# A hybrid decoder step on one core: the tanh-GELU of its state-space branch with the cubic constant inside ScalarE's square, and one VectorE instruction where two instructions stood

## The chip, the core and the metric

The program runs on one core of a Trainium2 chip: TensorE (PE in the profile; its weight loads are PEld), VectorE (DVE), ScalarE (ACT), GpSimd (POOL), and SyncE (SP), which issues most of the transfers. The metric is the device time of one execution in microseconds, lower is better. A difference of 0.2%, about 6 us, is what a measurement of this kernel can just tell from no change.

## The reference, cut to what matters

The reference is one layer of a decoder over a prompt of 2048 tokens and 32 sample tokens (8 sequences of 4). A combined projection feeds two branches, a diagonal state-space branch (S5) and a retention branch. Both feed an output projection; a memory cross-attention and a squared-ReLU MLP follow. The change concerns the activation of the state-space branch, the tanh form of GELU:

```python
y = y.reshape(bsz, L, SSM_WIDTH) + d_skip.astype(F32) * uf
z = jax.nn.gelu(y)
out = z * jax.nn.sigmoid(z @ w_glu.astype(F32))
```

With x the branch's output, GELU is 0.5 x (1 + tanh(0.798 (x + 0.044715 x³))). The kernel holds x/4 in the tile `yS`, so the inner term is built as y · (1 + 0.044715 (4y)²) and scaled by 4 · 0.798 in the tanh.

## The kernel before

The prompt is cut into four blocks of 512 tokens; the sample tokens ride along in the second block, whose tiles are 544 columns wide. The program first runs a **mixer phase** over the four blocks (block 0 to block 3 in what follows), then the attention and MLP phase over the same blocks. Every large matrix product is made of three fp32r products with the operands split into a high and a low part. Weights come in as `raw`, ScalarE copies out the high part and VectorE or GpSimd computes the low part (both go into the tile `whl`), and the product lands in a PSUM tile `dn`.

In the mixer phase each block has four groups of channels in its S5 branch, called batches here, so 16 in all. A batch (`s5_batch`) transposes its input to `u4`, multiplies by the matrices `q4` (PSUM tiles `vr`, `vi`), rotates the products on VectorE and GpSimd (tiles `t0`, `t1`, `gl`, which the profile shows as `t` and `gl`), runs two scans (`Yr`, `Yi`), rotates back, and multiplies by `pm4` into the PSUM tile `py`. ScalarE evicts `py`, TensorE transposes it (`pf`), ScalarE writes `yS`, and `s5_gelu` is started. Its tile `gl = mb(..., "yT")` is called `yT` in the profile. Its last two steps split the result into the tile `z`.

Beside the S5 batches run the four retention heads of the block: projections evicted as `qr`, `kr`, `gate` on VectorE and GpSimd, a transpose `pkd`, scores `psc`, the state product `pkv`, the output `po`, normalised in `scs`, and a transpose `pt`. The retention of the sample tokens, one head after the other, uses the small tiles `rsc`, `px`, `po2`, `pn` (the products `pn` update the sample state; `rsc` is their masked operand, built on GpSimd). Each engine runs its instructions in the order written.

That order is not written out by hand: the program carries a small planner (`Model`, `Order`). It keeps a clock per engine, adds for each instruction a start cost and a cost per column, and lets side jobs (`s5_chain`, `s5_gelu`, `retention`, `ret_sample`) go on when its clock says that they are due; `yield "sg1"` and the like give the offset in ns by which a job waits after its own last instruction. With the key set to 2, `E("x_g1")` gives the instruction to whichever of VectorE and GpSimd the planner thinks is free first. So an instruction less in a side job moves that job's due time, and with it the place of other jobs' instructions on all engines.

Of the kernel before, what the change touches and what calls it, by code (L numbers as in the profile page):

```python
# [13 lines left out]
AF = mybir.ActivationFunctionType  # L14
ALU = mybir.AluOpType
# [313 lines left out]
def tile_decoder_step(ctx: ExitStack, tc: tile.TileContext, ins: dict, outs: dict):  # L329
    nc = tc.nc  # L330
    model = Model()
    V, A, G, SY = (Engine(model, e, k) for e, k in ((nc.vector, "V"), (nc.scalar, "A"), (nc.gpsimd, "G"), (nc.sync, "SP")))
    T = nc.tensor

    def E(key):
        return Either(model, (V, G), key)
# [73 lines left out]
    def zact():  # L410
        return com.tile([P, 2, TM_], F32R, tag="z", name="z", bufs=4)
# [51 lines left out]
    def split(dst, src, scale=None):  # L463

        split_first(dst, src, scale)
        split_rest(dst, src, scale)
# [564 lines left out]
    def mb(shape, tag, bufs=1, dt=F32):  # L1031
        return pt("mixb", shape, tag, bufs, dt)
# [271 lines left out]
    def s5_batch(B, be, mats, nxt):  # L1304
# [82 lines left out]
        if sample:  # L1387
# [12 lines left out]
            for tt_ in range(4):  # L1400
                tr(pfs[:, tt_ * NB:(tt_ + 1) * NB], yTs[:, tt_].rearrange("p a b -> p (a b)"), ident[:NB, :NB])
            A.activation(yS[:, :, P:], pfs[:, :4 * NB].rearrange("p (a b) -> p a b", a=4), AF.Copy)
        M["gelu"] = od.spawn(s5_gelu(B, yS), yS)

    def s5_gelu(B, yS):
        t = B["t"]
        y = yS[:, :, :t // 4]
        gl = mb((P, 4, TM_ // 4), "yT")[:, :, :t // 4]
        A.activation(gl, y, AF.Square, scale=4.0)
        E("x_g1").tensor_scalar(gl, gl, 0.044715, 1.0, op0=ALU.mult, op1=ALU.add)  # L1410
        E("x_g2").tensor_tensor(out=gl, in0=gl, in1=y, op=ALU.mult)
        yield "sg1"
        A.activation(gl, gl, AF.Tanh, scale=4.0 * 0.7978845608028654)
        yield "sg2"
        V.scalar_tensor_tensor(out=gl, in0=gl, scalar=1.0, in1=y, op0=ALU.add, op1=ALU.mult)
        while B["b"] and "glu" not in blk[B["b"] - 1]:
            yield 300
        z = zact()
        split(z[:, :, :t].rearrange("p s (a b) -> p s a b", a=4), gl)
        B["z"].append(z)  # L1420
# [954 lines left out]
```

## Time and profile before

| | |
|---|---|
| device time, median of 3 runs | 3053.83 us (3050.05 to 3056.23) |
| the profiled execution: its time, and its span from first to last instruction | 3057.99 us, 3055.8 us |
| PE busy | 2944.5 us, 96% of the span |
| DVE, POOL, ACT busy | 1767.3 us, 1314.5 us, 1007.1 us |
| TensorE's granted clock over the span | 0.988 |

Busy shares are averages over phases with different limits: TensorE is the bound of the whole, and what the other engines do matters where TensorE waits for them. The mixer phase, in which all 16 GELUs lie, ends at about 960 us.

### The profile page before, as it was taken

What the parts mean: (1) busy time and instruction counts of PE and PEld (TensorE: products, weight loads), DVE (VectorE), ACT (ScalarE), POOL (GpSimd) and SP (SyncE); (2) the same over time, 40 slices, a digit from 0 to 9 for tenths busy, and PEclk for the clock granted to TensorE, in tenths of its full rate; (3) what the DMA queues carried; (4) which work ended last, traced back from release to release, by engine and by line L of the source; (5) the groups of instructions that cost most, each with busy time, mean ns of one, the idle gap of its engine ahead of it and who ended that gap; (6) DMA issues with size and microseconds to landing.
All of it is one profiled execution on the core that took longest, in us unless ns stands there. A gap on an engine that the chain in (4) does not pass through costs nothing.

```text
span 3055.8 us, 43238 instructions
## 1 busy us (share of the span) xinstructions
PE 2944.5 (96%) x16676; PEld 2561.3 (84%) x16676; DVE 1767.3 (58%) x3088; ACT 1007.1 (33%) x1440; POOL 1314.5 (43%) x1463
## 2 busy tenths in 40 slices
PE   8898899998989999999999999999999999999998
PEld 6688788877987978888987888788999998978887
DVE  8968858779675654334465555556533444553334
ACT  4442232322454332223333333433322223432222
POOL 5534434344565153334534344462433326153334
PEclk9999999999999999999999999999999999999999
DMA  5453253342685222234324444542222233232222
GB/s 151 137 171 111 83 154 119 115 156 75 230 269 168 90 93 95 96 97 141 114 88 145 145 149 148 198 134 83 91 84 90 90 132 122 81 99 94 96 90 76
DMA packets 138957, 374.37 MB, mean 123 GB/s; under 512 B 18656, under 2 KB 39808, under 8 KB 138752
## 3 DMA queue, kind: packets, MB, share of 16 engines
q1 hardware_dynamic: 138176, 371.10, 37.3%
q8 instruction: 131, 2.15, 0.3%
q14 instruction: 74, 0.61, 0.1%
q10 hardware_dynamic: 576, 0.52, 0.1%
HBM read 334.17 MB, written 37.40 MB: 122 GB/s over the span
## 4 chain that ended last, share of the span: by engine, by line
PE 65%; DVE 1%; issue 0%; DMA 0%; ACT 0%; POOL 0%; POOLq 0%; SPq 0%; ACTq 0%; DVEq 0%
PE dn L447 57%; PE sc L447 6%; PE zps L447 1%; DVE rst L197 1%; PE ptp L451 0%; PE st L447 0%; DVE rsy L197 0%; DMA raw<-in_w_down 0%; DVE act L197 0%; PE sp L447 0%; POOL x L197 0%; DVE mx L197 0%; ACT x L197 0%; DVE stage L197 0%; DVE ms L197 0%
## 5 line engine op out<-in xcount | busy, mean ns | idle before, releaser
L447 PE MATMUL dn<-actl,whl 128*128 128x512 f32 (+2 forms) x4656 | 916.3, 356 | 2.2 <-DVE x L197 2.2
L447 PE MATMUL dn<-act,whl 128*128 128x512 f32 (+2 forms) x4704 | 913.3, 348 | 2.1 <-POOL whl L197 1.6
L197 POOL TENSOR_TENSOR whl<-raw,whl 128x256 fp32r<-128x256 f32 x896 | 692.7, 805 | 510.8 <-ACT whl L197 494.3
L447 PEld LDWEIGHTS dn<-actl,whl 128*128 128x128 f32 x4656 | 767.7, 188 | 130.5 <-ACT whl L197 1.9
L447 PEld LDWEIGHTS dn<-act,whl 128*128 128x128 f32 x4704 | 752.7, 189 | 110.8 <-issue 3.0
L197 ACT ACTIVATE whl<-raw 128x1024 fp32r<-128x1024 f32 (+1 forms) x505 | 523.2, 1046 | 650.7 <-PE dn L447 460.5
L197 DVE TENSOR_TENSOR x<-dn,x 128x512 f32<-128x512 f32 (+2 forms) x496 | 291.4, 606 | 430.7 <-PE dn L447 430.2
L197 DVE TENSOR_TENSOR whl<-raw,whl 128x1024 fp32r<-128x1024 f32 (+1 forms) x281 | 400.0, 1429 | 174.3 <-ACT whl L197 164.2
L447 PE MATMUL dn<-z,whl 128*128 128x512 f32 (+1 forms) x2160 | 435.1, 352 | 0.0
L447 PEld LDWEIGHTS dn<-z,whl 128*128 128x128 f32 x2160 | 353.4, 188 | 56.5 <-issue 1.1
L197 POOL TENSOR_TENSOR actl<-sq,actl 128x512 fp32r<-128x512 f32 (+1 forms) x128 | 171.2, 1338 | 455.0 <-DVE sq L197 445.4
L197 DVE SCALAR_TENSOR_TENSOR relu<-dn,rb 128x512 f32<-128x512 f32 (+1 forms) x160 | 91.6, 589 | 323.4 <-PE dn L447 316.0
L197 ACT ACTIVATE actl<-relu 128x512 fp32r<-128x512 f32 (+1 forms) x128 | 82.2, 642 | 512.5 <-DVE relu L197 512.5
L447 PE MATMUL dn<-whl,act 128*128 128x512 f32 x768 | 203.0, 413 | 11.6 <-ACT whl L197 6.3
L197 POOL TENSOR_TENSOR acc<-acc,relu 128x512 f32<-128x512 f32 (+2 forms) x77 | 107.4, 1394 | 237.1 <-ACT relu L197 235.0
L447 PEld LDWEIGHTS dn<-whl,act 128*128 128x128 f32 x768 | 168.0, 255 | 35.9 <-ACT whl L197 7.0
L197 DVE TENSOR_TENSOR sq<-relu 128x512 f32<-128x512 f32 (+1 forms) x128 | 91.6, 715 | 14.8 <-POOL actl L197 2.3
L447 PE MATMUL sc<-whl,act 128*128 128x256 f32 x576 | 80.3, 291 | 14.2 <-ACT p L197 9.4
L447 PEld LDWEIGHTS sc<-whl,act 128*128 128x128 f32 x576 | 75.1, 197 | 15.6 <-ACT p L197 10.0
L447 PE MATMUL sc<-whl,z 128*128 128x256 f32 x576 | 80.8, 291 | 0.0
L197 DVE SCALAR_TENSOR_TENSOR act<-x,small,act 128x512 fp32r<-128x512 f32 (+2 forms) x76 | 64.4, 854 | 28.2 <-ACT act L197 28.2
L197 ACT ACTIVATE act<-x,small 128x512 fp32r<-128x512 f32 (+2 forms) x76 | 53.0, 701 | 72.8 <-DVE x L197 52.9
(318 smaller groups left out, 2671.8 us busy)
## 6 DMA issues: line engine op xcount, KB each, us to landing
raw<-in_w_up SPq DMA_DIRECT2D x128, 512.0 KB, 3.5
raw<-in_w_down SPq DMA_DIRECT2D x128, 512.0 KB, 3.5
raw<-in_w_out SPq DMA_DIRECT2D x32, 512.0 KB, 3.5
raw<-wq_d SPq DMA_DIRECT2D x32, 512.0 KB, 3.5
raw<-wo_d SPq DMA_DIRECT2D x32, 512.0 KB, 3.5
x<-in_xT SPq DMA_DIRECT2D x48, 256.0 KB, 4.3
pm<-pm_d SPq DMA_DIRECT2D x16, 768.0 KB, 5.3
tab<-tab_d SPq DMA_DIRECT2D x16, 516.0 KB, 4.4
```

The lines of the kernel that those rows point to most:

```text
L197: return f(*args, **kw)
L447: T.matmul(out, lhsT, rhs, start=start, stop=stop)
```

## The change

ScalarE's square takes the scale 4·√0.044715 in place of 4, so that it gives 0.044715 (4y)². The multiply-add by a tensor-scalar instruction and the multiplication by y, two instructions that the planner gives to VectorE or GpSimd, become one VectorE instruction, (square + 1) · y.

```diff
@@ s5_gelu
         gl = mb((P, 4, TM_ // 4), "yT")[:, :, :t // 4]
-        A.activation(gl, y, AF.Square, scale=4.0)
-        E("x_g1").tensor_scalar(gl, gl, 0.044715, 1.0, op0=ALU.mult, op1=ALU.add)
-        E("x_g2").tensor_tensor(out=gl, in0=gl, in1=y, op=ALU.mult)
+        A.activation(gl, y, AF.Square, scale=4.0 * 0.044715 ** 0.5)
+        V.scalar_tensor_tensor(out=gl, in0=gl, scalar=1.0, in1=y, op0=ALU.add, op1=ALU.mult)
         yield "sg1"
         A.activation(gl, gl, AF.Tanh, scale=4.0 * 0.7978845608028654)
```

By the change 16 instructions go, 13 of them on VectorE and 3 on GpSimd. In the planner's new order the engines' programs are the same up to about 217 us and from about 960 us on; between them the order differs in places. Three of those follow.

The first place is VectorE and TensorE in the first S5 batch of block 1. The rows of VectorE before, from the rotation of `vr` to the scans (the second `SCALAR_TENSOR_TENSOR yT` is (tanh + 1)·y):

```order
L197 TENSOR_TENSOR gl<-vr,tab 128x4x128
L197 TENSOR_SCALAR yT<-yT 128x544
L197 TENSOR_TENSOR yT<-yT,yS 128x544
L197 TENSOR_TENSOR t_4392<-vi,tab 128x4x128
L197 COPY Yr<-carr 128x4
L197 COPY Yi<-cari 128x4
L197 TENSOR_TENSOR kr<-dn,cosr 128x512
L197 TENSOR_TENSOR tmp<-dn,sinr 64x512 x2
L197 SCALAR_TENSOR_TENSOR yT<-yT,yS 128x544
L197 TENSOR_TENSOR z<-yT,z 128x544
L197 SCALAR_TENSOR_TENSOR Yr<-rho_86,carr,t_4391 128x128 x4
```

VectorE now:

```order
L197 TENSOR_TENSOR gl<-vr,tab 128x4x128
L197 SCALAR_TENSOR_TENSOR yT<-yT,yS 128x544
L197 TENSOR_TENSOR t_4388<-vi,tab 128x4x128
L197 COPY Yr<-carr 128x4
L197 COPY Yi<-cari 128x4
L197 SCALAR_TENSOR_TENSOR yT<-yT,yS 128x544
L197 TENSOR_TENSOR z<-yT,z 128x544
L197 TENSOR_TENSOR kr<-dn,cosr 128x512
L197 TENSOR_TENSOR tmp<-dn,sinr 64x512 x2
L197 SCALAR_TENSOR_TENSOR Yr<-rho_86,carr,t_4387 128x128 x4
```

The end of the GELU has moved ahead of the eviction of `kr`. On TensorE the same stretch, one piece of the difference:

```order
-L447 MATMUL dn<-act,whl 128x512 x36
-L451 MATMUL pkd<-ident,kr 128x128 x4
-L447 MATMUL psc<-qr,kr 128x128 x4
-L447 MATMUL dn<-act,whl 128x512 x6
+L447 MATMUL dn<-act,whl 128x512 x39
+L451 MATMUL pkd<-ident,kr 128x128 x4
+L447 MATMUL psc<-qr,kr 128x128 x4
+L451 MATMUL pu<-ident,tm_3965 128x128 x4
+L447 MATMUL dn<-act,whl 128x512 x6
```

Three more of the projection's matmuls stand ahead of `pkd`; further on, between `po` and the next batch's `py`, 9 stand where 15 stood, so `py` comes three matmuls earlier.

The second place is GpSimd and TensorE in block 0, where the sample state of the first head is updated. GpSimd before, from the first `rsc` of that head to the last:

```order
L197 TENSOR_TENSOR rsc<-vs,svec 96x256
L197 TENSOR_TENSOR whl<-raw,whl 128x256 x4
L197 TENSOR_TENSOR kr<-kr,tmp 128x272 x2
L197 COPY keep<-kr 128x32
L197 TENSOR_TENSOR rsc<-vs,svec 96x256
L197 TENSOR_TENSOR whl<-raw,whl 128x256 x4
L197 TENSOR_TENSOR rsc<-vs,svec 96x256
L197 TENSOR_TENSOR gl<-Yi,tab 128x516
L197 TENSOR_TENSOR Yi<-Yi,tab 128x516
L197 TENSOR_TENSOR rsc<-vs,svec 96x256
```

GpSimd now:

```order
L197 TENSOR_TENSOR kr<-kr,tmp 128x272 x2
L197 COPY keep<-kr 128x32
L197 TENSOR_TENSOR whl<-raw,whl 128x256 x4
L197 MEMSET ve_2654 128x1
L197 TENSOR_TENSOR rsc<-vs,svec 96x256
L197 TENSOR_TENSOR gl<-Yi,tab 128x516
L197 TENSOR_TENSOR Yi<-Yi,tab 128x516
L197 TENSOR_TENSOR rsc<-vs,svec 96x256 x2
```

The first `rsc` now stands behind `kr` and four weight pieces, and the second behind two rotations of the S5 batch. TensorE's products `pn` on these, before:

```order
L447 MATMUL pn<-rsc,kd_2479 128x256
L447 MATMUL dn<-act,whl 128x272 x36
L451 MATMUL pkd<-ident,kr 128x128 x4
L447 MATMUL psc<-qr,kr 128x128 x4
L447 MATMUL pn<-rsc,kd_2479 128x256
L451 MATMUL pu<-ident,tm_1745 128x128 x4
L447 MATMUL dn<-act,whl 128x272 x6
L447 MATMUL pkv<-tm_2065,kd 128x128 x4
```

And now:

```order
L447 MATMUL dn<-act,whl 128x272 x18
L451 MATMUL pkd<-ident,kr 128x128 x4
L447 MATMUL psc<-qr,kr 128x128 x4
L447 MATMUL pn<-rsc,kd_2564 128x256
L447 MATMUL dn<-act,whl 128x272 x6
L447 MATMUL pn<-rsc,kd_2564 128x256
L447 MATMUL pkv<-tm_2064,kd 128x128 x4
L447 MATMUL pn<-rsc,kd_2564 128x256
```

The first `pn` has moved from ahead of `pkd` to right behind the scores, with six matmuls to the second.

The third place is ScalarE in the first batch of block 2 (`tm_...` is the evicted S5 input). Before:

```order
L197 ACTIVATE tm_5990<-dn,rsy 128x512 x2
L197 ACTIVATE whl<-raw 128x1024
L197 ACTIVATE yT<-yT 128x4x128
L197 ACTIVATE z<-yT 128x512
L197 ACTIVATE whl<-raw 128x1024
```

And now:

```order
L197 ACTIVATE tm_5982<-dn,rsy 128x512 x2
L197 ACTIVATE yT<-yT 128x4x128
L197 ACTIVATE whl<-raw 128x1024
L197 ACTIVATE z<-yT 128x512
L197 ACTIVATE whl<-raw 128x1024 x2
```

The tanh (`yT<-yT`) has moved ahead of a weight copy.

## Rows read from the trace of the kernel before

**Rows 1.** The page: busy time by engine, and the chain that ended last.

```profile
PE 2944.5 (96%) x16676; PEld 2561.3 (84%) x16676; DVE 1767.3 (58%) x3088; ACT 1007.1 (33%) x1440; POOL 1314.5 (43%) x1463
...
PE 65%; DVE 1%; issue 0%; DMA 0%; ACT 0%; POOL 0%; POOLq 0%; SPq 0%; ACTq 0%; DVEq 0%
```

**Rows 2.** Busy us by stretch: PE, PEld, DVE, ACT, POOL, then clock, DMA.

```profile
200.00:400.00 200.00, 177.53 (x1196) 160.52 (x1197) 153.77 (x363) 55.16 (x82) 95.01 (x118) 0.97 0.36 119
400.00:612.00 212.00, 204.49 (x1206) 178.35 (x1205) 157.45 (x322) 68.37 (x105) 79.36 (x75) 1.00 0.40 122
612.00:790.00 178.00, 163.42 (x860) 140.06 (x859) 140.42 (x276) 51.62 (x78) 82.29 (x78) 0.98 0.37 121
790.00:960.00 170.00, 159.60 (x1047) 143.57 (x1048) 114.12 (x163) 82.92 (x127) 98.61 (x106) 0.99 0.75 253
960.00:3056.00 2096.00, 2063.12 (x11545) 1794.02 (x11543) 1028.43 (x1545) 664.73 (x928) 856.46 (x974) 0.99 0.33 110
```

**Rows 3.** The tile yT: ns of one, min/median/max, then first and last start.

```profile
L197 DVE TENSOR_TENSOR yT<-yT,yS x16: 672/693/1280, 219.0 to 949.7; 128x512 f32<-128x512 f32 x12, 128x544 f32<-128x544 f32 x4
...
L197 DVE SCALAR_TENSOR_TENSOR yT<-yT,yS x16: 672/710/1787, 225.0 to 952.5; 128x512 f32<-128x512 f32 x12, 128x544 f32<-128x544 f32 x4
...
L197 DVE TENSOR_SCALAR yT<-yT x13: 414/1205/1227, 217.8 to 908.8; 128x512 f32<-128x512 f32 x9, 128x544 f32<-128x544 f32 x4
...
L197 POOL TENSOR_SCALAR yT<-yT x3: 620/1133/1262, 303.0 to 948.5; 128x512 f32<-128x512 f32 x3
```

**Rows 4.** DVE by groups, 210 to 960 us: busy us, mean ns, idle before.

```profile
L197 DVE TENSOR_SCALAR yT<-yT 128x512 f32<-128x512 f32 (+1 forms) x13 | 12.6, 971 | 0.0
```

**Rows 5.** Timeline of DVE, block 1: start us, us, what, idle before.

```profile
460.19 1.23 DVE L197 TENSOR_SCALAR yT<-yT 128x544 f32<-128x544 f32 x1
...
463.12 0.69 DVE L197 TENSOR_TENSOR kr<-dn,cosr 128x512 f32<-128x512 f32 x1 [0.20 <-PE dn L447]
```

**Rows 6.** Timeline of PE, block 1.

```profile
465.67 1.54 PE L447 MATMUL dn<-act,whl 128*128 128x512 f32 x6
...
479.93 0.71 PE L447 MATMUL py<-pm,t 128*128 128x128 f32 x4 [1.41 <-DVE t L197]
```

**Rows 7.** Timelines of ACT, DVE and PE, block 2.

```profile
648.57 0.62 ACT L197 ACTIVATE yT<-yT 128x512 f32<-128x512 f32 x1
...
648.71 1.39 DVE L197 TENSOR_TENSOR whl<-raw,whl 128x1024 fp32r<-128x1024 f32 x1 [0.92 <-ACT whl L197]
...
663.30 0.66 PE L451 MATMUL pkd<-ident,kr 128*128 128x128 f32 x4 [1.75 <-POOL kr L197]
...
711.93 1.22 DVE L197 TENSOR_SCALAR yT<-yT 128x512 f32<-128x512 f32 x1
...
725.12 0.66 PE L451 MATMUL pkd<-ident,kr 128*128 128x128 f32 x4 [2.05 <-POOL kr L197]
```

**Rows 8.** Timelines of POOL and PE, block 0.

```profile
277.00 2.78 POOL L197 TENSOR_TENSOR whl<-raw,whl 128x256 fp32r<-128x256 f32 x4
279.74 0.73 POOL L197 TENSOR_TENSOR rsc<-vs,svec 96x256 fp32r<-96x256 f32 x1
280.83 1.19 POOL L197 TENSOR_TENSOR gl<-Yi,tab 128x516 f32<-128x516 f32 x1 [0.36 <-DVE Yi L197]
282.10 1.53 POOL L197 TENSOR_TENSOR Yi<-Yi,tab 128x516 f32<-128x516 f32 x1
...
276.03 0.44 PE L451 MATMUL pkd<-ident,kr 128*128 128x128 f32 x2 [0.94 <-POOL kr L197]
276.30 1.34 PE L447 MATMUL psc<-qr,kr 128*128 128x128 f32 x8
...
281.39 1.16 PE L447 MATMUL pkv<-tm,kd 128*128 128x128 f32 x8 [1.28 <-DVE scs L197]
...
285.40 0.49 PE L447 MATMUL po<-tm,scs 128*128 128x128 f32 x2 [1.98 <-DVE s L197]
```

**Rows 9.** The columns of Rows 2, one short stretch.

```profile
276.93:280.34 3.41, 3.17 (x15) 2.85 (x14) 3.41 (x2) 0.86 (x2) 3.41 (x6) 0.50 0.00 0
```

## The prediction

> **What bounds the kernel.** I read the page first. TensorE is busy 96% of the span and holds 65% of the chain that ended last, the other engines about 1% [rows 1]. So the other engines count only where TensorE waits for them. Then I asked for the busy times in five stretches: the mixer phase of each block, and the rest [rows 2]. The reader is to subtract PE's busy time from the length. TensorE stands idle 22.5 us in block 0 (200 to 400 us), 7.5 in block 1, 14.6 in block 2, 10.4 in block 3, and 32.9 us after 960 us, where the change leaves every engine's order alone. The change can therefore only win from, or add to, some 55 us of waits. DVE is busy 153.8 of 200 us, 157.5 of 212, 140.4 of 178 and 114.1 of 170 in the four blocks. It is the busiest engine behind TensorE, but it has free time too. Time freed on DVE reaches the end only where DVE works without a pause from the GELU to something that TensorE waits for. So I then followed single GELUs in the timeline.
>
> **What is removed, and its price.** The 13 TENSOR_SCALAR instructions on DVE took 12.6 us together [rows 4], and the three on POOL 0.62 + 1.13 + 1.26 = 3.0 us (minimum, median and maximum of three are all of them) [rows 3]. Their DVE price is uneven, 0.41 us at least and 1.21 in the median, so most were held up by something; I take the sum as it stands. The 16 TENSOR_TENSOR of the product become 16 SCALAR_TENSOR_TENSOR with the same operands. The kernel already runs that very instruction on the same tiles as the last step of the GELU: 672 ns at least against 672, 710 in the median against 693 [rows 3]. I price the exchange at nothing; the bounds are the largest single values, 1.79 us against 1.28, at most 0.5 us for each of 16. ScalarE's square keeps its shape and its price, since only a constant changes.
>
> [...]
>
> **Where the freed time goes.** The planner moves other work by what it thinks was freed, so each place has to be walked.
>
> Block 1 (four batches of one pattern). Before, the TENSOR_SCALAR ran at 460.19 for 1.23 us, and DVE then waited only 0.20 us, for TensorE at `kr` [rows 5]. In the new order the GELU's end fills that place and `kr` follows it. From there the timeline has DVE without a pause up to `t<-t,gl`, but for the one inside the GELU, and for that operand `py` waits 1.41 us [rows 6]. So that operand is ready about 1.15 us earlier: 1.23 and the 0.20, less some 0.3 that I allow, as an estimate, for DVE waiting on ScalarE inside the GELU, which now stands closer together. The bounds are 0 and 1.43. But TensorE also comes to `py` earlier, by three matmuls. Six of them show as 1.54 us [rows 6], so three are 0.77. The wait goes from 1.41 to 1.41 - 1.15 + 0.77 = 1.03 us, a gain of 0.4. Two batches have this wait: **-0.8 us**. For the other two I take 0.
>
> Block 2. In the first batch DVE comes to its next weight piece 0.92 us early already [rows 7], so the freed time ends in that idle. Worse, ScalarE now does the tanh, 0.62 us, ahead of the weight copy on which that piece waits. DVE is 0.62 us late from there on, and behind it is `kr`, for which TensorE waits 1.75 us already [rows 7]: +0.6. In the third batch the TENSOR_SCALAR took 1.22 us, and the next `pkd` waited 2.05 us for `kr` [rows 7]; I let all 1.2 through. The two other GELUs of the block I count at 0.25 each, between 0 and the row's minimum of 0.41. Together **-1.1 us**.
>
> Block 3. TensorE idles 10.4 us here, with DVE busy in 67% of the time [rows 2]. Three TENSOR_SCALAR at the median would be 3.6 us. Most of that will fall into idle time, so between 0 and 3.6 I take **-0.5 us**.
>
> Block 0. This is where the order changes most, and it is the step that can cost. The first `pn` of the first head now stands right behind the scores, while its `rsc` on POOL stands behind `kr` and four weight pieces. Once `kr` is there, POOL needs 2.78 + 0.73 = 3.5 us [rows 8]; TensorE's scores take 1.34 of that. That is a new wait of about 2.2 us. The second `rsc` then stands behind two rotations: 1.19 + 1.53 + 0.73 = 3.45 us, against `pn` (256 columns) and six matmuls of 272 columns on TensorE. From the 1.54 us for six of 512 columns [rows 6] I estimate these at 0.3 and 0.8, so another 2.3. Queued behind these are `pkv` and `po`, and for those TensorE waited 1.28 and 1.98 us before [rows 8]. DVE now has these 4.5 us to get them ready, so I let those 3.3 us vanish. Net **+1.2 us**. The remaining waits of this block are dealt anew; I see no sign in them, and allow 4 us either way.
>
> The sum is -0.8 - 1.1 - 0.5 + 1.2 = -1.2 us. The profiled execution took 3057.99 us, of which 3055.8 are its span and 2.2 lie around it; that is 4.2 us above the median of the runs shown. Counted against it the sum gives 3056.8, and against the median 3052.6 us.
>
> **The rivals.** *The freed time arrives* (faster). If most of the 12.6 us reaches TensorE, the time is 3053.8 - 12.6 = 3041; from half of it on, 3047.5, the verdict turns. For it: DVE is busy 74 to 79% in blocks 0 to 2, and short waits on it fill that time. [...] Against it: the planner gives TensorE the earlier place at the same time, as in block 1, and the first GELU of block 2 shows the time dying in idle.
>
> *The sample state's products wait* (slower). If the waits on `rsc` in block 0 come without the relief behind them they cost 4.5 us, and if each is followed by a stretch of low clock as above, 3.4 more. That is 7.9 us, or 3061.7, where nothing is gained elsewhere, and 5.5 with the 2.4 of blocks 1 to 3. It decides from 6.1 us on. For it: the new order on POOL is plain, with 2.78 us of weight pieces in front. Against it: `pkv` and `po` are queued behind `pn` on TensorE, so that old waits are met inside the new ones.
>
> [...]
>
> **How the numbers follow.** No change within 0.2% (3047.7 to 3059.9) as forecast: 0.50; the half-rate case, which ends there too: 0.02. The freed time arrives: 0.27. The waits on `rsc` decide: 0.21. The time is the likeliest case's, 3052.6. The range reaches to 3043, where five sixths of the freed time arrive, and up to 3062, the whole of the slower rival and the spread of the runs; outside I leave about 2 in 10. The forecast's own range is 3047.7 to 3059.9. Faster 0.27, same 0.52, slower 0.21.
>
> **What would show it.** [...] PE idle from 960 us on within 2 us of 32.9. `py` in block 1 waiting about 1.0 us where it waited 1.41. `pkd` at the first batch of block 2 waiting longer than 1.75 us and at the third less than 2.05. In block 0 waits of `pn` on POOL `rsc` of about 2 us each. I am wrong if PE's idle time in the four blocks moves by more than 6 us from 55.0, and the block in which it does so names the step.

## The result and the profile after

The change made the kernel slower: 3070.1 us in the median of four runs (3069.2 to 3071.5), against 3053.6 us beside it. The ratio is 1.0054, with a 95% interval of 1.0042 to 1.0066; that is 16.5 us. The prediction said 3052.6 us, in a range up to 3062. The profiled execution took 3069.64 us, 3067.9 of them its span.

A word on "block" first. The retention heads beside the S5 batches of a block are those of the next block, not of the same one: the rows of block 0 hold `kr` in two pieces of 272 columns and a `gate` of 544, which is the width of block 1. So block 0 below means the S5 branch of block 0 with the heads and the sample tokens of block 1, and so on.

I cut both traces at the same matmuls, the product `sp` of the normalisation at each block's end (after block 3 the `st` ahead of it). The windows of the kernel before come first: length, busy us of PE, PEld, DVE, ACT and POOL with their instructions, then the granted clock and the DMA.

```profile
196.20:423.90 227.70, 205.22 (x1336) 183.97 (x1335) 170.62 (x396) 62.78 (x94) 102.14 (x124) 0.98 0.40 122
423.90:620.60 196.70, 189.19 (x1132) 164.94 (x1130) 151.17 (x315) 62.26 (x94) 77.61 (x73) 1.00 0.38 123
620.60:792.40 171.80, 156.94 (x820) 134.50 (x818) 134.96 (x266) 50.89 (x77) 80.72 (x77) 0.98 0.36 116
792.40:991.80 199.40, 184.48 (x1168) 164.46 (x1169) 133.03 (x171) 95.47 (x146) 118.21 (x122) 0.98 0.68 230
991.80:3049.00 2057.20, 2035.54 (x11413) 1771.02 (x11412) 1005.87 (x1523) 651.02 (x907) 834.77 (x956) 0.99 0.33 110
```

The same windows of the changed kernel, and three short ones inside block 0:

```profile
193.40:429.30 235.90, 212.02 (x1337) 190.68 (x1336) 171.73 (x395) 62.55 (x94) 96.73 (x121) 0.93 0.39 118
429.30:633.00 203.70, 190.99 (x1133) 166.17 (x1131) 154.89 (x309) 62.28 (x94) 79.58 (x75) 0.99 0.36 119
633.00:802.50 169.50, 157.76 (x820) 136.02 (x818) 131.42 (x263) 51.42 (x77) 77.71 (x76) 0.97 0.36 117
802.50:1003.60 201.10, 186.29 (x1168) 165.11 (x1169) 134.77 (x166) 95.18 (x146) 120.91 (x123) 0.97 0.67 229
1003.60:3061.10 2057.50, 2036.48 (x11414) 1768.64 (x11412) 1004.63 (x1523) 650.36 (x907) 833.76 (x956) 1.00 0.32 110
279.15:285.98 6.83, 5.14 (x22) 4.99 (x23) 6.14 (x18) 0.00 (x0) 2.93 (x6) 0.50 0.20 59
299.63:306.46 6.83, 4.75 (x21) 3.52 (x21) 4.17 (x14) 2.29 (x4) 1.31 (x2) 0.50 0.17 55
320.11:326.94 6.83, 5.31 (x23) 5.31 (x24) 6.25 (x14) 1.06 (x1) 3.71 (x5) 0.50 0.10 40
```

Block 0 grew by 8.2 us and block 1 by 7.0; block 2 shrank by 2.3, block 3 grew by 1.7, and the rest of the program is as long as it was. The two large losses are of different kinds. In block 1 TensorE's idle time (length less busy) grew from 7.5 to 12.7 us. In block 0 it hardly grew, from 22.5 to 23.9 us; there the same 1336 or 1337 matmuls took 6.8 us longer. The clock column goes with it: 0.93 in place of 0.98. From these I estimate, with the rest at 1.00, about 2 · 0.07 · 235.9 = 33 us at the lower level (0.50) in place of 9. Three of these stretches are the short windows.

TensorE's own timeline of the changed kernel shows what stands ahead of them (start, length, matmuls, and in brackets the idle time before and what ended it), and then a wait of block 1 and two of block 2:

```profile
280.84 0.55 PE L447 MATMUL pn<-rsc,kd 96*128 96x256 f32 x1 [3.69 <-DVE oN L197]
...
300.90 1.12 PE L451 MATMUL pt<-ident,scs 128*128 128x128 f32 x4 [5.45 <-DVE scs L197]
...
321.63 0.58 PE L447 MATMUL pn<-rsc,kd 96*128 96x256 f32 x1 [3.94 <-POOL rsc L197]
...
483.29 0.49 PE L447 MATMUL po<-Sv,qr 128*128 128x128 f32 x2 [2.24 <-DVE Sv L197]
...
674.91 0.98 PE L451 MATMUL pkd<-ident,kr 128*128 128x128 f32 x4 [2.11 <-POOL kr L197]
...
736.53 1.12 PE L451 MATMUL pkd<-ident,kr 128*128 128x128 f32 x4 [2.27 <-POOL kr L197]
```

Before, no wait of block 0 was longer than 2.4 us. The view of waits on TensorE (total us, times, longest) has this one as the longest:

```profile
PE pkv L447 <- DVE scs L197: 3.7, 2, 2.4
```

Now the idle time is much the same, but three waits hold 13.1 us of it, and in each of the three a stretch of 6.83 us at half clock begins (277.15 to 280.84, 295.45 to 300.90 and 317.69 to 321.63 us, against the starts of the short windows).

DVE's timeline of the changed kernel shows how two of the losses come about: the 5.45 us in block 0, and the first batch of block 1.

```profile
292.55 0.36 DVE L197 BATCH_NORM_AGGREGATE mv<-bs 128x2 f32<-128x6 f32 x4
...
293.45 0.69 DVE L197 TENSOR_TENSOR t<-vr,tab 128x512 f32<-128x512 f32 x1 [0.40 <-issue]
294.35 0.69 DVE L197 TENSOR_TENSOR t<-vi,tab 128x512 f32<-128x512 f32 x1 [0.20 <-PE vi L447]
294.96 0.68 DVE L197 TENSOR_TENSOR gl<-vr,tab 128x512 f32<-128x512 f32 x1
295.56 1.48 DVE L197 SCALAR_TENSOR_TENSOR gate<-gth,gate 128x544 f32<-128x544 f32 x1
296.96 0.22 DVE L197 TENSOR_SCALAR ve<-mv,rvec 128x4 f32<-128x4 f32 x1
...
465.59 1.51 DVE L197 SCALAR_TENSOR_TENSOR yT<-yT,yS 128x544 f32<-128x544 f32 x1
...
467.83 1.82 DVE L197 SCALAR_TENSOR_TENSOR yT<-yT,yS 128x544 f32<-128x544 f32 x1
470.38 0.73 DVE L197 TENSOR_TENSOR z<-yT,z 128x544 fp32r<-128x544 f32 x1 [0.72 <-ACT z L197]
471.02 0.68 DVE L197 TENSOR_TENSOR kr<-dn,cosr 128x512 f32<-128x512 f32 x1
...
482.96 0.27 DVE L197 SCALAR_TENSOR_TENSOR Sv<-S,pkv 128x128 f32<-128x128 f32 x1
```

The same places before:

```profile
288.30 0.36 DVE L197 BATCH_NORM_AGGREGATE mv<-bs 128x2 f32<-128x6 f32 x4
...
288.89 0.23 DVE L197 TENSOR_SCALAR ve<-mv,rvec 128x4 f32<-128x4 f32 x1
...
473.14 0.27 DVE L197 SCALAR_TENSOR_TENSOR Sv<-S,pkv 128x128 f32<-128x128 f32 x1
```

In block 0 the S5 batch now comes earlier, and its three rotation products, with the `gate`, stand between `mv` and `ve`. So `ve` starts 4.05 us behind the end of `mv`, where it started 0.23 us behind before, and the normalisation that follows it, on whose `scs` TensorE waits, is late by that. In block 1 the end of the GELU fills the place ahead of `kr`, as foreseen. But `kr` started 2.93 us after the GELU's first instruction before [rows 5], and starts 5.43 us after it now. What reads `kr` is late in turn: `pkd`, `psc`, and on DVE what stands behind, the state `Sv` among it, for which `po` now waits. `Sv` starts 17.37 us after the GELU's first instruction, where it was 12.95. Of these 4.42 us the late `kr` is 2.50; in the rest the two scans ahead of `Sv` take 5.89 us for 4.50, and the rotation `t<-Yr`, which stood behind `Sv`, now stands ahead of it.

The tile `yT` itself, in the view by instruction (ns of one: minimum, median, maximum):

```profile
L197 DVE SCALAR_TENSOR_TENSOR yT<-yT,yS x32: 656/694/1825, 214.6 to 961.8; 128x512 f32<-128x512 f32 x24, 128x544 f32<-128x544 f32 x8
```

### The profile page after: what moved, and what is told of

Its sections match the earlier page's. It is cut to its first block, busy times and chain, and to the rows that moved or that the text cites. A ratio compares the mean times of both kernels' runs of the same rounds, so it can differ in the third digit from the quotient of the medians.

```text
span 3067.9 us, 43235 instructions
## 1 busy us (share of the span) xinstructions
PE 2954.7 (96%) x16676; PEld 2567.2 (84%) x16676; DVE 1767.4 (58%) x3073; ACT 1006.4 (33%) x1440; POOL 1309.1 (43%) x1462
## 4 chain that ended last, share of the span: by engine, by line
PE 65%; DVE 1%; issue 0%; DMA 0%; ACT 0%; POOL 0%; POOLq 0%; SPq 0%; ACTq 0%; DVEq 0%
PE dn L447 57%; PE sc L447 6%; PE zps L447 1%; DVE rst L197 1%; PE ptp L451 0%; PE st L447 0%; DVE rsy L197 0%; DMA raw<-in_w_down 0%; PE sp L447 0%; POOL x L197 0%; DVE act L197 0%; DVE mx L197 0%; ACT x L197 0%; DVE stage L197 0%; PE pq L451 0%
```

## The experiments

Theory: the new order lost the time, block by block, and the new instruction by itself costs nothing or gains. Rivals: the instruction is slower than it looked; the loss is a matter of the single execution; it hangs on one wait. The kernel before was timed anew beside each set of experiments (medians of 3057.2 to 3060.1 us), so only ratios are compared; 0.1% is 3.05 us. A difference of two such ratios is uncertain by some 0.18%, or 5 to 6 us (their two intervals combined). The expectations' times are meant on the scale of 3053.6 us.

### Order and instruction apart

First the fused instruction with the planner charged as before. This gives the order of before on all five engines, with one instruction where two stood:

```diff
+    def plan2(o, ins, name):     # charge V or G as Either would
...
-        V.scalar_tensor_tensor(out=gl, in0=gl, scalar=1.0, in1=y, op0=ALU.add, op1=ALU.mult)
+        plan2(gl, [gl], "tensor_scalar")
+        plan2(gl, [gl, y], "tensor_tensor")
+        V.eng.scalar_tensor_tensor(out=gl, in0=gl, scalar=1.0, in1=y, op0=ALU.add, op1=ALU.mult)
```

> The new instruction in the old order: the planner is charged for the two old instructions, and one SCALAR_TENSOR_TENSOR is issued at the place of the old product, so that all five engines keep the order of before. Theory 1, the new order lost the time: no loss here, and of the 7.7 us that DVE is busy less on these tiles little reaches TensorE: 3049 to 3054 us. Rival, the new instruction itself is the loss, since it took 1.5 us in half of the batches: 3062 us or more.

Measured 0.9985 (0.9972 to 0.9998): 4.6 us faster than before, and only just clear of no change. Then the reverse, the two old instructions on DVE with the planner charged for one, which gives the order of the changed kernel:

```diff
-        A.activation(gl, y, AF.Square, scale=4.0 * 0.044715 ** 0.5)
-        V.scalar_tensor_tensor(out=gl, in0=gl, scalar=1.0, in1=y, op0=ALU.add, op1=ALU.mult)
+        A.activation(gl, y, AF.Square, scale=4.0)
+        model.done("V", "scalar_tensor_tensor", [gl], [gl, y])
+        V.eng.tensor_scalar(gl, gl, 0.044715, 1.0, op0=ALU.mult, op1=ALU.add)
+        V.eng.tensor_tensor(out=gl, in0=gl, in1=y, op=ALU.mult)
```

> The two old instructions in the new order: the planner is charged for the one new instruction, and TENSOR_SCALAR and TENSOR_TENSOR are issued on DVE at its place. Theory 1, the order lost the time: 3070 us at least, and a few us more where the longer pair is in the way, 3070 to 3080. Rival, the new instruction is the loss: back to about 3054 us.

Measured 1.0073 (1.0058 to 1.0087). The four cases agree: the new order costs 0.69% with the new instruction (1.0054 less 0.9985) and 0.73% with the old ones, 21 and 22 us; the instruction gains 0.15% in the old order and 0.19% in the new, 4.6 and 5.8 us. The loss is the order's: 21 us is far outside the uncertainty. The instruction's gain is only just clear of zero in the old order, and at the edge of it in the new.

### Block by block

Next the new instruction everywhere, but the planner charged for it in some blocks only (and as before in the others). The order then differs from that of before only in the blocks named.

```diff
+        if B["b"] in (0,):          # then (1,), then (2, 3)
...
+            V.scalar_tensor_tensor(out=gl, in0=gl, scalar=1.0, in1=y, op0=ALU.add, op1=ALU.mult)
+        else:
...
+            plan2(gl, [gl], "tensor_scalar")
...
```

> The new instruction in all four blocks, the new order in block 0 alone. By the two traces block 0 lost 8.2 us: theory 1 expects 3058 to 3062 us, with half-clock stretches of some 34 us together between 200 and 430 us. If block 0's extra time belongs to the execution and not to the order, as the old order before would: 3050 to 3054 us.

> The new instruction in all four blocks, the new order in block 1 alone. By the two traces block 1 lost 7.0 us: theory 1 expects 3057 to 3061 us, with TensorE waiting 1.4 to 2.8 us for Sv in three batches. If the loss of block 1 was a consequence of block 0's: 3050 to 3054 us.

> The new instruction in all four blocks, the new order in blocks 2 and 3 alone. With the runs on block 0 (0.35% above the new instruction in the old order) and on block 1 (0.19%) the three should add up to the 0.69% between that run and the changed kernel: some 0.15% is left for blocks 2 and 3, so 3052 to 3056 us. Rival, blocks 0 and 1 hold all of it: 3048 to 3051 us.

Measured 1.0020 (1.0006 to 1.0034), 1.0004 (0.9992 to 1.0016) and 0.9994 (0.9982 to 1.0007). Against the 0.9985 of the new instruction in the old order these are 10.7, 5.8 and 2.7 us, together 19.2 of the 21 us. On the scale of 3053.6 us they are 3059.7, 3054.8 and 3051.8 us: the first as forecast, the second below its 3057 to 3061 and the third just below its 3052 to 3056. By time alone block 1's 5.8 us are barely clear of zero and the 2.7 us of blocks 2 and 3 are not; for block 1 the trace decides. The waits come back one by one. Block 0's order alone, in the view of waits on TensorE (total us, times, longest):

```profile
PE pt L451 <- DVE scs L197: 7.8, 2, 5.4
PE pn L447 <- DVE oN L197: 5.2, 1, 5.2
PE pn L447 <- POOL rsc L197: 4.1, 2, 3.7
```

Its block 0 took 234.8 us at a clock of 0.93, while block 0 of the kernel with the new instruction in the old order took 228.3 at 0.97.

This is no matter of one execution. I cut block 0 in the same way in ten of the profiled executions of this study. In the five with its old order (before, the new instruction in the old order, the new order in block 1 or in blocks 2 and 3 alone, and the last version below) it took 226.5 to 228.5 us, with 10 to 21 us at half clock and TensorE busy for 205.2 to 209.3 us. In five with its new order it took 234.8 to 239.7 us, with 31 to 34 us at half clock and TensorE busy for 210.4 to 213.1 us. Idle time is part of it too: 19.2 to 21.2 us in the four of the old order that have the new instruction, 23.3 to 24.8 in the new order with it. So with the same instruction the order costs block 0 some 4 us of waits and some 5 us of slower matmuls; against the 22.5 us that TensorE idled before, the waits hardly show.

Block 1's order alone shows the waits on `Sv` of the changed kernel to the tenth:

```profile
PE po L447 <- DVE Sv L197: 6.5, 3, 2.8
...
PE pkd L451 <- POOL kr L197: 3.7, 4, 1.4
```

Block 1 took 203.7 us in this run, as in the changed kernel, behind a block 0 of 226.5. So its loss is no consequence of block 0's.

### The place in block 1

The changed kernel with the GELU's second offset at 600 for 300 in block 1 alone: its second instruction and the split of `z` go back behind `kr`.

```diff
-        yield "sg2"
+        yield "sg2" if B["b"] != 1 else "sg2b"      # "sg2b": 600
```

> The changed kernel with that same offset at 600 in block 1 alone: there the GELU's second instruction and the split of `z` go back behind `kr` and its two products, and blocks 0, 2 and 3 keep the new order but for what follows from it. Theory, block 1 lost its 7 us because the GELU's end was put ahead of `kr`: 5 to 7 us less than the changed kernel, 3063 to 3065 us where that takes 3070, and TensorE's waits for Sv gone. Rival, the waits for Sv come from elsewhere: unchanged.

Measured 1.0034 (1.0022 to 1.0047), 0.20% or 6.1 us less than the changed kernel's ratio. In the view of waits only these two are left in block 1, as before the change:

```profile
PE py L447 <- DVE t L197: 6.9, 4, 3.2
PE dn L447 <- DVE tm L197: 1.9, 1, 1.9
```

The waits on `Sv` are gone. But more than one place went back: with this offset the block's order on TensorE and VectorE is nearly all that of before, `gate` and `Sv` ahead of `t<-Yr` included. So the run shows that this block's new order costs its time; that the place of `kr` alone does is not shown. In its profiled execution the block took 200.2 us, 3.5 less than in the changed kernel, which agrees with 6.1 us within the uncertainty.

### Places and waits in block 0

In block 0 the first long wait, at `pn`, ended with DVE's `oN`, and DVE had waited 3.42 us for a memset of `ve` that stood on POOL behind four weight pieces (2.80 us). I moved the memset to DVE and kept the order:

```diff
-            G.memset(ve2, 1.0)
+            model.done("G", "memset", [ve2], [])
+            V.eng.memset(ve2, 1.0)
```

> The changed kernel, its order kept, with the four small memsets of the sample state's `ve` issued on DVE and not on POOL. In the changed kernel's block 0 the memset stood on POOL behind four weight pieces of 2.80 us, DVE waited 3.42 us for it, and TensorE 3.69 us at `pn`. Theory: that wait goes (below 0.7 us, then limited by `rsc`) and some of the half-clock time behind it: 3 to 6 us less than the changed kernel, 3064 to 3067 us where that takes 3070. Rival, `pn` waits for `rsc` on POOL whatever DVE does: wait and time unchanged, 3069 to 3071.

Measured 1.0063 (1.0047 to 1.0079), or 3072.8 us: no gain, and outside both forecasts. DVE's timeline of this run tells where it went:

```profile
278.38 0.06 DVE L1576 MEMSET ve<- 128x1 f32 x1
...
278.90 0.16 DVE L197 TENSOR_TENSOR rst<-rsy 128x1 f32<-128x1 f32 x1
279.10 0.64 DVE L197 SCALAR_TENSOR_TENSOR rst<-rst,ve 128x1 f32<-128x1 f32 x1
...
281.82 1.68 DVE L197 SCALAR_TENSOR_TENSOR rst<-rst 128x1 f32<-128x1 f32 x1
...
283.97 0.40 DVE L197 TENSOR_SCALAR oN<-po,mv,rsy 32x128 f32<-32x128 f32 x1
```

DVE no longer waits, but five of its tiny instructions, 0.16 us elsewhere, take 0.64 to 1.68 us. By the order kept, POOL's weight pieces and the two instructions that follow them fall beside these five; that they held them up is my estimate. TensorE's 3.69 us became 1.82 at the first `pn` and 1.18 at the second. My theory of this wait fell: with the memset out of the way the same chain ran slower, and two waits of 3.0 us together stand where one of 3.69 did. The half-clock stretch behind them stayed as well (285.15 to 291.98 us).

Two runs then tested the low clock. Useless matmuls (their results are overwritten) were put on TensorE ahead of the `pt` and the `pn` that waited 5.45 and 3.94 us:

```diff
         pt_ = aux("pt")
+        if B["sample"] and h == 1:
+            for c in range(5):
+                T.matmul(pt_, ident, rmask.rearrange("p a b -> p (a b)"), start=True, stop=True)
...
-                pn = aux("pn")[:, :2 * P]
+                pn = aux("pn")
+                if h == 1 and i == 2:      # three matmuls of the same kind into pn
...
```

> The changed kernel, its order kept, with eight matmuls of no use put on TensorE in two of block 0's long waits: five of 512 columns ahead of the transpose `pt` that waited 5.45 us, three ahead of the `pn` that waited 3.94 us. Their results are overwritten. Theory, the waits cost twice because the granted clock falls to half for 6.83 us behind each: with TensorE busy in them those two stretches go, 3 to 6 us less than the changed kernel, 3064 to 3067 us where that takes 3070. Rival, the low clock is not brought on by the waits, or the useless work is in the way: unchanged or slower, 3069 us or more.

> The fill again, so placed that it can start in the wait. In the last run the first five useless matmuls waited for DVE's `scs` themselves, 5.44 us, and then cost 7.22 us. Here they write to a tile that was read long before, and nothing holds them; four stand ahead of the `pn`. Theory, the low clock follows the two waits: the stretches of 6.83 us behind both go or shorten, block 0 holds 20 to 27 us of half clock where it held 34, and takes 2 to 5 us less than the changed kernel's 235.9 us; the time 3065 to 3068 us where that takes 3070. Rival, the low clock comes with this order whatever TensorE does in the waits: 34 us of half clock as before, block 0 at 236 us or more.

Measured 1.0081 (1.0065 to 1.0096) and, with the five written to an older tile, 1.0073 (1.0053 to 1.0094): both no faster than the changed kernel (the first is 0.27% slower), and the forecast times missed. At `pt` the fill failed both times. In the first run the useless matmuls waited 5.44 us themselves; in the second the wait, 6.59 us now, moved to an earlier `px`. Either way 7.22 and 6.36 us of useless work came on top. At `pn` it worked, as the second run's TensorE shows:

```profile
324.62 3.60 PE L1592 MATMUL pn<-rmask,ident 128*128 128x512 f32 x8
328.74 0.38 PE L447 MATMUL pn<-rsc,kd 96*128 96x256 f32 x1 [0.52 <-POOL rsc L197]
```

Its windows, behind the wait that was not filled and from the one that was:

```profile
298.61:308.85 10.24, 5.63 (x14) 3.42 (x15) 6.61 (x24) 2.29 (x4) 2.34 (x5) 0.50 0.18 68
...
324.62:335.00 10.38, 8.81 (x46) 5.86 (x44) 10.21 (x19) 1.16 (x2) 6.54 (x9) 1.00 0.07 26
```

Where TensorE was kept busy in the wait the half-clock stretch is gone; where it still waited there is one, of 10.24 us where it was 6.83 in the changed kernel. In the first run six matmuls of 272 columns behind the filled `pn` took 0.92 us, as in the second (0.91, at 1.00), where they took 1.57 in the changed kernel (at 0.50): the stretch is gone there too. In the second run the half-clock time of block 0 came to 27 us, the upper end of its forecast, but the block took 240.0 us. That the low clock follows the long waits is supported by these runs; that filling pays is not. Nor is it shown that it takes a long wait: in the last version below, block 0 in its old order has a stretch of 10.24 us at half clock (277.43 to 287.67 us) behind waits none of which is longer than 1.4 us.

### Does any new deal lose?

The kernel before with its two instructions and one offset changed (`sg1` 350 to 950), the changed kernel with `sg2` 300 to 600 everywhere, and last the new instruction in the old order but for block 2, where the new charge goes with `sg2` 600:

> The kernel before, its two instructions kept, with one offset of the planner changed (the tanh due 600 ns later, 950 for 350): the order is dealt anew in the same phase, in about two thirds as many rows as by the change. Theory, the order of before is one that the offsets were chosen for, and any new deal loses: slower by 5 to 20 us, 3059 to 3074 us. Rival, only the places that the change moved are bad, and a deal is as often better as worse: within 5 us of before on either side.

> The changed kernel with the other offset of the GELU at 600 for 300, so that the planner lets the second instruction come later: less than half as many rows then differ from the order of before (143 on DVE, where the change has 364). Theory, the order decides: most of the loss goes, 3050 to 3060 us. Rival, the loss lies in few places that this does not touch: 3065 us or more.

> The new instruction in all blocks, the old order in blocks 0, 1 and 3, and in block 2 the new order with the GELU's second offset at 600. That block took 166.3 us in the run with this offset everywhere, 169.3 in the run of the new instruction in the old order, and 171.7 before. If block lengths add: 3 us less than the old order gave, 3045 to 3048 us, which would beat both kernels. Rival, these 3 us were a matter of the clock in one execution: 3049 us.

Measured 1.0037 (1.0021 to 1.0053), 1.0037 (1.0023 to 1.0052) and **0.9974 (0.9964 to 0.9985)**. A new deal with not one instruction changed costs 11 us, so a loss of this kind needs no fault in the new instruction. The second, 3064.9 us on the scale of 3053.6, missed its 3050 to 3060 us. But a new deal may also win: with `sg2` at 600 everywhere block 2 took 166.4 us, against 169.3 in the old order, both at a clock of 0.99. Its window in that run:

```profile
631.70:798.10 166.40, 154.56 (x820) 132.73 (x818) 130.84 (x263) 51.47 (x77) 78.31 (x76) 0.99 0.37 119
```

TensorE's idle time there is 11.8 us, against 14.3 in the old order. Block 0 of that run still took over 235 us, which is why it lost as a whole. Put together with the old order in the other blocks it is the fastest version of this study, 0.26% or 8 us faster than before and 0.80% faster than the changed kernel; block 2 took 166.3 us there, again with 11.8 us idle. Against the new instruction in the old order, 0.9985, it is 0.11% faster in time, which is within the uncertainty: the gain of this deal rests on the two traces.

## Why the prediction was wrong

**The step that failed** is the sentence on block 0, "The remaining waits of this block are dealt anew; I see no sign in them, and allow 4 us either way". It cost 8.2 us in the traces, and its order alone 10.7 us in the timed runs. What the runs showed in its place: three waits of 13.1 us together, and some 33 us at half clock where there were 9. I had followed two products of the sample state and left the rest as noise without sign. The rest was many times the net 1.2 us that I worked out, and part of it could have been read from the order: three rotation products of the S5 branch ahead of a normalisation on DVE.

**What "can change".** "The change can therefore only win from, or add to, some 55 us of waits" was wrong too. Over the four blocks TensorE's idle time went from 59.8 to 63.1 us (the windows above), only 3.4 us. My own test, idle time moving by more than 6 us, would have called the prediction right. The busy time moved: the matmuls of block 0 ran 6.8 us longer, those of the other three blocks 4.4 us together. I had put the low clock into a rival only, at 3.4 us for two waits: for each, half of the 3.41 us at 0.50 in [rows 9]. No run shows that term; the trace of the changed kernel showed three stretches of 6.83 us instead, and some 33 us at half clock in block 0 altogether. And [rows 8] and [rows 9] already showed those 3.41 us beginning 0.90 us behind the end of a wait of 0.94 us.

**Block 1**, -0.8 us forecast, cost 7.0 in the traces and 5.8 in its own run, and is the second step that failed. The forecast saw the move, `kr` behind the GELU's end, but followed only one operand, `py`'s. That wait did shrink, and by more than I had said. The view of waits, before and after:

```profile
PE py L447 <- DVE t L197: 6.7, 4, 3.2
...
PE py L447 <- DVE t L197: 1.2, 2, 0.7
```

The longest, 3.17 us, was in one of the two batches for which I took 0. But `kr` has readers of its own: the waits on `Sv`, 6.5 us, and of `pkd`, 3.4 us, are new. The 0.3 us that I had allowed for DVE waiting on ScalarE inside the closer GELU did not come (0.72 us, and 0.73 before); what came was that its two instructions ran at 1.51 and 1.82 us beside POOL. The run that put the GELU's end back behind `kr` has neither wait.

**Blocks 2 and 3**, -1.1 and -0.5 us forecast, gave -2.3 and +1.7 in the traces, and together +2.7 in their run, whose interval spans some 4 us either way. The two `pkd` of block 2 went from 1.75 to 2.11, as said, and from 2.05 to 2.27, where I had said less.

**The freed time** was mis-sized. I took 12.6 us off DVE; its work on `yT` fell from 12.6 + 12.6 us for the old pair to 18.5 for the new instruction in the old order, so 6.7 us. The price "nothing" for the exchange was too low by 0.37 us on average, inside the bound of 0.5. What reached the end in the old order, 4.6 us (0.6 to 8.5 by its interval), is if anything more than the forecast gave it: its sum of gains in blocks 1 to 3 was 2.4.

**The half-rate case**, the new instruction at twice the time of the old one, had 0.02 of the chances. No run shows it: of the 32 SCALAR_TENSOR_TENSOR on `yT` in the changed kernel 21 took 0.66 to 0.73 us. The other 11 took 1.46 to 1.83 us, twice as long or more, but each of these started 0.04 to 0.37 us behind a product of POOL, and of the 21 only one started well inside one (at 257.10 us, beside a product of 2.95 us). In the old order the 16 new instructions took 0.67 to 1.79 us, 1.47 in the median. That nine of them meet a product of POOL so is my estimate, from the nine TENSOR_SCALAR that did before (1.20 to 1.23 us each, 0.37 us behind a product).

**What held:** the TENSOR_SCALAR are gone, the median is 0.69 us, ScalarE's square kept its price (0.63 us in the median before and after), and the program behind block 3 kept its idle time (21.7 and 21.0 us). `pkv` and `po` behind the first `pn` did shed their waits (none and 0.51 us). Of the two waits of `pn` one came, larger (3.69 us) and by another road; the second came a head later, 3.94 us on `rsc`.

## What to carry to other kernels

Where a planner deals out the order, an instruction less is two changes; measure them apart by charging the planner as before, and keep the gain without the deal. Follow every reader of an instruction that moves, not only the wait one is looking at, and do not give a part of the order no sign because it is long. Where the granted clock falls, as here to 0.50, sum up busy time as well as idle time: in block 0 a little more idle time, gathered into a few long waits, went with some 20 us more at half clock, and with slower matmuls.

## What the hardware showed that I had not expected

In two places of block 1, of DVE and POOL the one that started second took longer. POOL's product `t` started at 465.22 for 1.30 us and DVE's new instruction 0.37 us later; it ended 0.58 us after POOL's end and took 1.51 us, where at 571.42 us, with POOL idle, it took 0.71. At 505.49 DVE started 0.02 us ahead of POOL's next product: it took 0.72 us, and POOL 1.84 where that product took 1.29 at 467.78. POOL's rows of the changed kernel:

```profile
465.22 1.30 POOL L197 TENSOR_TENSOR t<-t,t 128x512 f32<-128x512 f32 x1 [4.38 <-DVE t L197]
467.78 1.29 POOL L197 TENSOR_TENSOR t<-t,gl 128x512 f32<-128x512 f32 x1 [1.26 <-DVE t L197]
...
505.51 1.84 POOL L197 TENSOR_TENSOR t<-t,gl 128x512 f32<-128x512 f32 x1 [2.40 <-DVE t L197]
```

The TENSOR_SCALAR before [rows 3] show the like of the first place: the nine of 1.20 to 1.23 us each started 0.37 us behind a product of POOL, the four of 0.41 to 0.44 us behind none. So I take their 1.2 us to have been in good part a toll of the place, which the next instruction in that place paid again: in the old order the 16 new instructions took 1.47 us in the median, and 1.79 at most.
